# Gated attention output stored as two scaled fp16 halves and read back by transposing DMAs, with the transform matrices and the split of the output weights reordered

## The chip, the cores and the metric

The kernel runs on one core of a Trainium2 chip. A core has a matrix engine (TensorE, PE in the profile), three engines for elementwise work (VectorE or DVE, ScalarE or ACT, GpSimd or POOL), an engine that only issues transfers here (SyncE, SP) and sixteen DMA engines. Each engine works through its own queue of instructions in order; semaphores hold an instruction back until what it reads is there and what it overwrites is no longer needed. The metric is the device time of one execution in microseconds; lower is better.

## The reference

One block of a hybrid encoder: an RMS norm, one input projection of 1024 to 6144 columns, a Fourier branch, a dilated window attention branch, and one output projection with a residual. Sequence 2048, model width 1024, all fp32.

```python
hn = rms_norm(h, norm_w)
proj = hn @ w_in
u_f, g_f, q, k, v, g_a = jnp.split(proj, SPLIT_POINTS, axis=-1)
f = jnp.fft.fft2(u_f, axes=(1, 3), norm="ortho").real       # per group of 64 columns
f = jnp.einsum('bsgc,gcd->bsgd', f, w_fourier)
y_f = f * jax.nn.silu(g_f)                                  # 512 columns
...
o = jnp.sum(alpha[..., None] * jnp.stack(outs, axis=0), axis=0)   # three dilations, weighted
y_a = o * jax.nn.silu(g_a)                                  # 512 columns
h = h + jnp.concatenate([y_f, y_a], axis=-1) @ w_out
```

## The kernel before

All fp32 products are made of three products of a high and a low half: each operand is split into `hi` (rounded to a narrower type) and `lo` (the rest), and TensorE adds hi x hi, hi x lo and lo x hi. A split is one copy on ACT (hi) and one subtraction on DVE (lo).

The program has four stages. First come 192 items of the q, k, v projection (a row tile of 128 positions each, `inproj`), with the attention of earlier tiles laced in (lines 300 to 560). Then 48 items of the rest of the input projection (`chan`, `tok`): the Fourier gate, stored in DRAM as `SG`; the Fourier input `u`, from which `u_out` makes four folded arrays `F`; and the attention gate in 16 items q = 0 to 15 of 256 rows by 256 columns. Beside these items a generator (`og_all`) loads the three attention outputs of item q (`ot`) and weights and adds them into a tile `yo`. `ga_out` (L713) reads the gate from PSUM, computes silu (two ACT operations, one on DVE), multiplies `yo` by it, and puts q on a list; one item later `ya_st` (L720) stores `yo` in the DRAM array `YA`, 2048 x 512 fp32.

The third stage, from L1220 (`tail_`), is the Fourier transform over the sequence, as four transforms s = 0 to 3. `f_trans(s)` multiplies `F[s]` by a small block matrix in four blocks (PSUM tile `ptr`), and ACT (L776) and DVE (L777) split the result into `at`. `f_dft(s)` multiplies `at` by the transform matrix `dt` in four blocks `ct` of 128 channels (PSUM tile `pf`); s = 0 and 1 (256 columns a half, L807) and s = 2 and 3 (512 columns, L812). For even s, ACT copies the PSUM to `pe` (L816). For odd s, DVE forms the sum `t1` (L823) and the difference in `pe` (L824), and these multiply the gate `Y`, loaded from `SG`: the lower half (L826) on GpSimd, on DVE for s = 3, and the upper half (L827) on GpSimd. The matrix of transform s is loaded raw (`d_dma`, tile `dr`, two buffers) and split (`d_split`, ACT L759, DVE L760). `w_out` is loaded in sixteen pieces of 128 x 512 (`wor`, three buffers, L862), eight for each half of the output columns, and split by `wo_prep` (ACT L872, DVE L873). Both splits are generators, and `f_trans` and `f_dft` take steps from them (`fill`) at fixed places: this sets where the splits stand in the queues of ACT and DVE.

The fourth stage is the output projection, `o_mm(r)` for 16 row tiles r: 48 matmuls of 512 columns (L922) on the operand `mx`, whose columns 4 to 7 come from `YA` and 0 to 3 from `Y`. Before the matmuls of row r TensorE transposes row r+1 of `YA` (`ya`) in four pieces of 128 x 128 (L899, PSUM tile `pya`), and ACT (L900) and DVE (L901) split it into `mx`; L906 and L908 split the part of `Y`. Row 0 is prepared inside `f_dft(3)` (`o_in0`, `o_mix_a(0)`) and `o_mix_y(0)`. `o_in(r)` loads `ya` and the residual `xo` two rows ahead.

Instructions of one engine stand in the order in which the code calls them.

Of the kernel before, what the change touches and what calls it, by code (L numbers as in the profile page):

```python
# [92 lines left out]
class Kernel:  # L93
# [503 lines left out]
    def silu(self, out, ps, sb, e, z):  # L597
        V, A = self.nc.vector, self.nc.scalar
        A.activation(e, ps, AF.Tanh, scale=sb[:, 3:4])
        A.activation(z, ps, AF.Copy, scale=sb[:, 3:4])  # L600
        V.scalar_tensor_tensor(out, e, 1.0, z, op0=OP.add, op1=OP.mult)
# [86 lines left out]
    def og_all(self):  # L688
        V = self.nc.vector
        for q in range(2):  # L690
            self.og_load(q)
        yield
        for Q in range(8):
            if Q < 7:
                self.og_load(2 * Q + 2)
# [15 lines left out]

    def ga_out(self, u, q):
        ps = self.PS.pop((u, q))  # L713
        y = self.YO[q].rearrange("p r w -> p (r w)")
# [2 lines left out]
        self.nc.vector.tensor_tensor(y, y, e[:, 0], OP.mult)
# [27 lines left out]
    def d_dma(self, s):  # L745
        self.DR = [self.dp.tile([128, 2, 512], F32, name="dr", tag="dr", bufs=2) for _ in range(2)]
        for q in range(2):
            n = 512 if s > 1 else 256
# [40 lines left out]
    def f_dft(self, s, fill=iter(())):  # L789
# [6 lines left out]
        for ct in range(4):  # L796
# [29 lines left out]
            (V if s == 3 else G).tensor_tensor(lo, lo, t1, OP.mult)  # L826
# [37 lines left out]
    def wo_prep(self, nh, wo):  # L864
        nc = self.nc
        V, A = nc.vector, nc.scalar
        for k in range(KT):
# [4 lines left out]
            A.copy(wo[k][:, 0], raw)  # L872
            V.tensor_tensor(wo[k][:, 1], raw, wo[k][:, 0].bitcast(F32), OP.subtract)  # L873
# [17 lines left out]
    def o_mix_a(self, r):  # L891
# [5 lines left out]
        ps = (self.pso, self.psp)[r % 2].tile([128, 4, 128], F32, name="pya", tag="op"[r % 2])  # L897
        for k in range(4):
            nc.tensor.transpose(ps[:, k], ya[:, k * 128:k * 128 + 128], self.idf)  # L899
# [380 lines left out]
```

## Time and profile before

Three runs took 1420.67, 1421.93 and 1424.03 us; the median is 1421.93.

| | us |
|---|---|
| profiled execution | 1421.88 |
| its span | 1420.1 |
| attention and q, k, v projection (to about) | 908 |
| rest of the input projection, to | 1165.9 |
| Fourier transforms, to | 1231.2 |
| output projection, matmuls to | 1416.5 |
| TensorE busy | 1389.2 |
| DVE, ACT, GpSimd busy | 988.3, 739.9, 459.8 |

The profile names engines as above; PEld is TensorE's loading of weights. A row of the timeline gives the start in us, the time taken, the engine, the line, the operation, what it writes and reads, and how many instructions are merged; in brackets stands the idle time of the engine just ahead of it and what ended that. An engine's queue of transfers is marked with a q (SPq). A row of a group gives busy time and the mean of one in ns. The granted clock is the share of full speed that TensorE was given.

### The profile page before, as it was taken

How to read it: one execution, taken by the hardware profiler on the slowest of the kernel's cores; microseconds unless marked ns; L12 is line 12 of the kernel's file. 1: busy time of each engine (PE TensorE's matmuls, PEld its weight loads, DVE VectorE, ACT ScalarE, POOL GpSimd, SP SyncE). 2: the span in 40 equal slices, each digit the busy share in tenths (PEclk: the TensorE clock that was granted, in tenths of full speed). 3: DMA queues.
4: the chain of work that ended last, by engine and by line, in shares of the span. 5: the costliest groups of instructions: out<-in, count | busy, mean ns of one | idle time of the engine just before them, and what ended most of it. 6: DMA issues, size and time to landing. Idle time of an engine off the chain costs nothing.

```text
span 1420.1 us, 27783 instructions
## 1 busy us (share of the span) xinstructions
PE 1389.2 (98%) x9570; PEld 1027.6 (72%) x9570; DVE 988.3 (70%) x3143; ACT 739.9 (52%) x2079; POOL 459.8 (32%) x637
## 2 busy tenths in 40 slices
PE   5999999999999999999999999999999997999998
PEld 3666666667777777778888888754458687788887
DVE  7888888888878888888777777744488676511111
ACT  6867766676757666666666666554213134300110
POOL 0255544444444444444433333320010002211110
PEclk9999999999999999999999999999999999999999
DMA  6876867776776777686756565554434336333332
GB/s 223 203 135 129 151 122 143 126 139 131 142 134 129 149 122 147 121 151 121 151 104 134 97 128 102 131 125 117 144 120 138 107 97 253 104 111 111 112 119 74
DMA packets 407374, 188.14 MB, mean 132 GB/s; under 512 B 302720, under 2 KB 388928, under 8 KB 406720
## 3 DMA queue, kind: packets, MB, share of 16 engines
q1 hardware_dynamic: 378628, 173.36, 54.8%
q10 hardware_dynamic: 28604, 13.00, 3.9%
q8 instruction: 75, 1.23, 0.4%
q14 instruction: 67, 0.55, 0.1%
HBM read 72.37 MB, written 29.76 MB: 72 GB/s over the span
## 4 chain that ended last, share of the span: by engine, by line
PE 84%; DVE 5%; DMA 4%; issue 2%; POOL 2%; ACT 1%; SPq 1%; POOLq 0%; DVEq 0%; ACTq 0%
PE psq L312 45%; PE py L922 12%; PE psq L574 12%; PE psq L590 6%; PE pS L461 4%; PE po L527 2%; DMA wor<-in_w_out_dram 2%; PE po L528 1%; PE pS L449 1%; DVE xhl L223 1%; POOL ph L509 1%; PE pya L899 0%; DVE wo L873 0%; POOL hl L376 0%; PE ptr L774 0%
## 5 line engine op out<-in xcount | busy, mean ns | idle before, releaser
L312 PE MATMUL psq<-wh,xT 128*128 128x384 f16 x4608 | 787.0, 327 | 3.3 <-ACT wh L289 1.5
L312 PEld LDWEIGHTS <-xT 128*128 128x128 f16 x4608 | 540.2, 119 | 193.8 <-issue 4.6
L497 ACT ACTIVATE P<-pS,ob,kb 128x256 f32<-128x256 f32 (+1 forms) x384 | 199.7, 527 | 150.4 <-DVE ob L489 150.1
L509 POOL TENSOR_TENSOR ph<-P,ph 128x512 f16<-128x512 f32 x160 | 189.1, 1182 | 195.1 <-ACT ph L504 183.5
L922 PE MATMUL py<-wo,mx 128*128 128x512 f32 x768 | 181.3, 395 | 0.3 <-DVE mx L901 0.3
L365 POOL TENSOR_TENSOR qn<-qn,kb 128x128 f32<-128x128 f32 x192 | 84.7, 441 | 294.0 <-DVE qn L364 205.1
L574 PE MATMUL psq<-xT,wh 128*128 128x512 f16 x768 | 168.9, 379 | 0.0
L479 DVE CUSTOM_DVE_ANT_0 pS<-pS,bt 128x256 f32<-128x256 f32 (+1 forms) x384 | 147.8, 385 | 27.2 <-PE pS L449 18.9
L922 PEld LDWEIGHTS py<-wo,mx 128*128 128x128 f32 x768 | 143.2, 188 | 32.3 <-DVE mx L901 0.8
L376 POOL TENSOR_TENSOR hl<-qn,hl 128x256 f16<-128x256 f32 x192 | 134.1, 698 | 30.7 <-ACT hl L371 30.7
L574 PEld LDWEIGHTS <-wh 128*128 128x128 f16 x768 | 74.2, 98 | 86.9 <-issue 0.8
L925 DVE TENSOR_TENSOR xo<-xo,py 128x512 f32<-128x512 f32 x32 | 22.0, 688 | 139.1 <-PE py L922 139.1
L538 DVE TENSOR_REDUCE ob<-po 128x128 f32<-128x256 f32 (+1 forms) x160 | 75.2, 470 | 54.3 <-PE po L528 54.3
L504 ACT CAST ph<-P 128x512 f16<-128x512 f32 x160 | 99.1, 619 | 8.0 <-ACT P L497 1.3
L371 ACT CAST hl<-qn 128x256 f16<-128x256 f32 x192 | 77.1, 401 | 47.3 <-POOL qn L365 37.5
L332 DVE TENSOR_TENSOR vt<-psq,vt 128x128 f16<-128x128 f32 x192 | 55.0, 286 | 59.0 <-ACT vt L331 59.0
L331 ACT CAST vt<-psq 128x128 f16<-128x128 f32 x192 | 51.2, 266 | 83.0 <-PE po L528 83.0
L291 DVE SCALAR_TENSOR_TENSOR wh<-wr,nws,wh 128x384 f16<-128x384 f32 x128 | 88.0, 694 | 5.7 <-ACT wh L289 5.7
L900 ACT CAST mx<-pya 128x512 fp32r<-128x512 f32 x16 | 9.4, 587 | 148.2 <-issue 124.9
L590 PE MATMUL psq<-wh,xT 128*128 128x256 f16 x768 | 84.3, 273 | 0.0
L590 PEld LDWEIGHTS <-xT 128*128 128x128 f16 x768 | 75.1, 98 | 9.1
L323 ACT COPY raw<-psq 128x256 f32<-128x256 f32 x192 | 69.5, 362 | 21.8 <-PE psq L312 21.4
(158 smaller groups left out, 1777.9 us busy)
## 6 DMA issues: line engine op xcount, KB each, us to landing
wr<-in_w_in_dram SPq DMA_DIRECT2D x104, 192.0 KB, 2.9
ot<-O SPq DMA_DIRECT2D x16, 792.0 KB, 4.5
st<-st SPq DMA_DIRECT2D x96, 128.0 KB, 2.4
xs<-in_x_dram SPq DMA_DIRECT2D x16, 512.0 KB, 7.3
xo<-in_x_dram SPq DMA_DIRECT2D x16, 512.0 KB, 3.5
out_dram<-xo SPq DMA_DIRECT2D x15, 512.0 KB, 2.9
O<-ob ACTq DMA_DIRECT2D x108, 66.0 KB, 2.5
O<-ob ACTq DMA_DIRECT2D x32, 132.0 KB, 2.9
```

Source lines behind the costliest of these rows:

```text
L291: V.scalar_tensor_tensor(wh[:, 1, k - 1, :n], wr[k - 1], nws[:, k - 1:k], wh[:, 0, k - 1, :n], op0=OP.mult, op1=OP.subtract)
L312: nc.tensor.matmul(ps[:, :384], self.xtile(j, k, c, t), wh[:, l, k, :384], start=n == 0, stop=n == 23)
L365: G.tensor_tensor(qn[:, 2:4], qn[:, 2:4], self.kf[:, h0:h0 + 2], OP.mult)
L371: self.nc.scalar.copy(hl.rearrange("p a h l d -> p (a h) l d")[:, :, 0], qn)
L376: self.nc.gpsimd.tensor_tensor(hv[:, :, 1], qn, hv[:, :, 0], OP.subtract)
L479: V.tensor_tensor_reduce(out=sS[:, h, cs], in0=ps[:, h, cs], in1=bs, scale=1.0, scalar=-3.0e38, op0=OP.add, op1=OP.max, accum_out=mx[:, e, ...
L497: self.nc.scalar.activation(P[:, h, cs], sS[:, h, cs], AF.Exp, bias=ob[:, e, 130 + h:131 + h], scale=self.om[:, h0 + h:h0 + h + 1], accum_ ...
L504: self.nc.scalar.copy(ph[:, 0], P)
L509: self.nc.gpsimd.tensor_tensor(ph[:, 1], P, ph[:, 0], OP.subtract)
L574: nc.tensor.matmul(ps, wh[:, l, k, col * 128:col * 128 + 128], self.xT[:, j, k, ch * 512:ch * 512 + 512], start=n == 0, stop=n == 23)
L590: nc.tensor.matmul(ps[:, j * 256:j * 256 + 256], self.xT[:, i, k, r * 128:r * 128 + 128], wh[:, l, k, 128:384], start=n % 24 == 0, stop=n ...
L922: nc.tensor.matmul(ps[nh], m[:, j, k], wo[nh][k][:, l], start=(j, l, k) == (0, 0, 4), stop=(j, k) == (1, 3))
```

## The change

The gated attention output is no longer stored as fp32. `ya_scale` computes, once for each half of the columns, a power of two from the bound on the values (five DVE operations on 128 x 1) and its inverse; silu's factor is multiplied by the one, and rows 4 to 7 of the pieces of `w_out` by the other when they are split. One item after `ga_out`, `ya_split` makes two fp16 halves of `yo` (a copy on ACT, a subtraction on DVE); one item later `ya_st` stores both in `YA`, now 2 x 2048 x 512 fp16. The last two items are split after the loop, ahead of the transforms.

In the output projection two transposing DMAs for each row tile load the halves of `ya` with the columns on the partitions; ACT and DVE copy them into `mx`, and the transposes on TensorE go.

The third matrix (s = 2) gets its own raw buffers and its own split tile; it is loaded first in the tail, ahead of the first two pieces of `w_out` and of `Y`. The steps of the splits are dealt out anew: matrix 1 in `f_trans(0)`, matrix 2 and two pieces of `w_out` in `f_dft(0)`, none in `f_trans(2)` and `f_dft(1)`, one piece in `f_trans(3)`, the rest from `f_dft(2)` on. In `f_dft(3)` the lower product of the first two blocks goes to GpSimd. `yo` has 6 buffers for 8, `t1` 3 for 2.

```diff
-    def silu(self, out, ps, sb, e, z):
+    def silu(self, out, ps, sb, e, z, zs=None):
...
-        A.activation(z, ps, AF.Copy, scale=sb[:, 3:4])
+        A.activation(z, ps, AF.Copy, scale=sb[:, 3:4] if zs is None else zs)
...
-        self.silu(e[:, 0], ps, self.W[u][1], e[:, 0], e[:, 1])
+        if q % 8 == 0:
+            self.ya_scale(q // 8, self.W[u][1])
+        self.silu(e[:, 0], ps, self.W[u][1], e[:, 0], e[:, 1], self.YS[q // 8][:, 2:3])
         self.nc.vector.tensor_tensor(y, y, e[:, 0], OP.mult)
+        self.YL.append(q)
+
+    def ya_split(self, q):
+        y = self.YO.pop(q).rearrange("p r w -> p (r w)")
+        h = self.YH[q] = self.gp.tile([128, 2, 512], F16, name="yh", tag="yh", bufs=2)
+        self.nc.scalar.copy(h[:, 0], y)
+        self.nc.vector.tensor_tensor(h[:, 1], y, h[:, 0], OP.subtract)
         self.YD.append(q)
+
+    def ya_scale(self, hf, sb):
+        V = self.nc.vector
+        t = self.YS[hf] = self.sm.tile([128, 3], F32, name="ysc", bufs=2)
+        V.tensor_reduce(t[:, 1:2], self.IS[:, hf].rearrange("p c s h -> p (c s h)"), AX.X, OP.max)
+        V.scalar_tensor_tensor(t[:, 1:2], t[:, 1:2], 2.0 ** 16, sb[:, 1:2], op0=OP.mult, op1=OP.mult)
+        V.tensor_scalar(t[:, 0:1].bitcast(I32), t[:, 1:2].bitcast(I32), 0x7F800000, None, op0=OP.bitwise_xor)
+        V.tensor_scalar(t[:, 1:2], t[:, 1:2], 0.5, None, op0=OP.mult)
+        V.tensor_tensor(t[:, 2:3], t[:, 0:1], sb[:, 3:4], OP.mult)
 
     def ya_st(self, q):
         hf, g = divmod(q, 8)
-        dst = self.YA[g * 256:g * 256 + 256, hf * 256:hf * 256 + 256].rearrange("(r p) w -> p r w", p=128)
-        self.nc.sync.dma_start(dst, self.YO.pop(q))
+        h = self.YH.pop(q)
+        for l in range(2):
+            dst = self.YA[l, g * 256:g * 256 + 256, hf * 256:hf * 256 + 256].rearrange("(r p) w -> p r w", p=128)
+            self.nc.sync.dma_start(dst, h[:, l].rearrange("p (r w) -> p r w", r=2))
...
     def d_dma(self, s):
-        self.DR = [self.dp.tile([128, 2, 512], F32, name="dr", tag="dr", bufs=2) for _ in range(2)]
+        self.DR[s] = [(self.fp if s == 2 else self.dp).tile([128, 2, 512], F32, name="dr", tag="dr", bufs=2) for _ in range(2)]
...
-        d = (self.dp2 if s % 2 else self.dp).tile([128, 2, 4, 512], F32R, name="dt", tag="dt", bufs=1)
+        w = 512 if s else 256
+        d = (self.dp2 if s else self.dp).tile([128, 2, 4, w], F32R, name="dt", tag="dt2" if s == 2 else "dt", bufs=1)
...
-            (V if s == 3 else G).tensor_tensor(lo, lo, t1, OP.mult)
+            (V if s == 3 and ct > 1 else G).tensor_tensor(lo, lo, t1, OP.mult)
...
-            A.copy(wo[k][:, 0], raw)
-            V.tensor_tensor(wo[k][:, 1], raw, wo[k][:, 0].bitcast(F32), OP.subtract)
+            if k < 4:
+                A.copy(wo[k][:, 0], raw)
+                V.tensor_tensor(wo[k][:, 1], raw, wo[k][:, 0].bitcast(F32), OP.subtract)
+            else:
+                sc = self.YS[k // 2 - 2][:, 1:2]
+                A.activation(wo[k][:, 0], raw, AF.Copy, scale=sc)
+                V.scalar_tensor_tensor(wo[k][:, 1], raw, sc, wo[k][:, 0].bitcast(F32), op0=OP.mult, op1=OP.subtract)
...
-            self.OI[r] = ya = self.yp.tile([128, 512], F32, name="ya", tag="ya", bufs=3)
-            nc.sync.dma_start(ya, self.YA[r * 128:r * 128 + 128])
+            self.OI[r] = ya = self.yp.tile([128, 2, 4, 128], F16, name="ya", tag="ya", bufs=3)
+            for l in range(2):
+                nc.sync.dma_start(ya[:, l], self.YA[l, r * 128:r * 128 + 128], transpose=True)
...
-        for k in range(4):
-            nc.tensor.transpose(ps[:, k], ya[:, k * 128:k * 128 + 128], self.idf)
-        A.copy(m[:, 0, 4:8], ps)
-        V.tensor_tensor(m[:, 1, 4:8], ps, m[:, 0, 4:8].bitcast(F32), OP.subtract)
+        A.copy(m[:, 0, 4:8], ya[:, 0])
+        V.tensor_copy(m[:, 1, 4:8], ya[:, 1])
...
+                yl, self.YL = self.YL, []
                 if prev:
                     prev()
+                for q in yl:
+                    self.ya_split(q)
...
-        self.Y_dma()
+        self.d_dma(2)
         for k in range(2):
             self.wo_load(0, k)
+        self.Y_dma()
         flush = lambda g: [None for _ in g]
-        self.f_trans(0)
+        s1, s2, s3 = self.d_split(1, 3), self.d_split(2), self.d_split(3)
+        self.f_trans(0, s1)
         self.f_trans(1)
         ny = self.f_nyq()
-        s1, s2, s3 = self.d_split(1, 2), self.d_split(2, 3), self.d_split(3)
-        self.f_dft(0, chn(s1, w0))
-        self.f_trans(2, w0)
+        self.f_dft(0, chn(s2, cut(w0, 2)))
+        self.f_trans(2)
         self.f_nyq_mul(ny)
-        self.f_dft(1, chn(s2, w0))
+        self.f_dft(1)
...
-        self.f_trans(3, w0)
+        self.f_trans(3, cut(w0, 1))
...
-        self.f_dft(2, chn(s3, w0, w1))
+        self.f_dft(2, chn(cut(w0, 3), s3, w0, w1))
         self.f_dft(3, w1)
```

The changed lines' numbers move: L777 becomes L798, L760 L781, L824 L845, L826 L847, L873 L895 (L899 where it scales), L901 L927, L854 L875.

DVE's queue from the third `f_trans` through `f_dft(1)`, before (`at` are the splits of `f_trans(2)`, `wo` those of `w_out`, `dt` that of the third matrix, `t` and `pe` the results of the blocks of `f_dft(1)`):

```order
L777 TENSOR_TENSOR at<-ptr,at 128x512 x4
L873 TENSOR_TENSOR wo_17214<-wor,wo_17214 128x512 x3
L854 TENSOR_TENSOR Y<-Y,pm 128x4
L823 TENSOR_TENSOR t_17456<-pe,pf 128x512
L824 TENSOR_TENSOR pe<-pe,pf 128x512
L760 TENSOR_TENSOR dt<-dr,dt 128x1024 x2
L823 TENSOR_TENSOR t_17483<-pe,pf 128x512
L824 TENSOR_TENSOR pe<-pe,pf 128x512
L873 TENSOR_TENSOR wo_17214<-wor,wo_17214 128x512
L823 TENSOR_TENSOR t_17505<-pe,pf 128x512
L824 TENSOR_TENSOR pe<-pe,pf 128x512
```

The same place now:

```order
L781 TENSOR_TENSOR dt<-dr,dt 128x1024 x2
L895 TENSOR_TENSOR wo_17290<-wor,wo_17290 128x512 x2
L798 TENSOR_TENSOR at<-ptr,at 128x512 x4
L875 TENSOR_TENSOR Y<-Y,pm 128x4
L844 TENSOR_TENSOR t_17521<-pe,pf 128x512
L845 TENSOR_TENSOR pe<-pe,pf 128x512
L844 TENSOR_TENSOR t_17539<-pe,pf 128x512
L845 TENSOR_TENSOR pe<-pe,pf 128x512
L844 TENSOR_TENSOR t_17557<-pe,pf 128x512
L845 TENSOR_TENSOR pe<-pe,pf 128x512
```

The third matrix's split and every split of `w_out` are gone from between the blocks.

DVE's queue around `f_dft(3)`, before (all but the last piece of `w_out` are split ahead of the first block):

```order
L873 TENSOR_TENSOR wo_17560<-wor,wo_17560 128x512
L823 TENSOR_TENSOR t_17662<-pe,pf 128x512
L824 TENSOR_TENSOR pe<-pe,pf 128x512
L826 TENSOR_TENSOR Y<-Y,t_17662 128x512
L873 TENSOR_TENSOR wo_17560<-wor,wo_17560 128x512
L823 TENSOR_TENSOR t_17685<-pe,pf 128x512
L824 TENSOR_TENSOR pe<-pe,pf 128x512
L826 TENSOR_TENSOR Y<-Y,t_17685 128x512
L823 TENSOR_TENSOR t_17703<-pe,pf 128x512
L824 TENSOR_TENSOR pe<-pe,pf 128x512
L826 TENSOR_TENSOR Y<-Y,t_17703 128x512
L901 TENSOR_TENSOR mx_17669<-pya,mx_17669 128x512
```

The same place now (`wo_17580` to `wo_17616` are the second half of `w_out`, L927 the low half of row 0's operand):

```order
L895 TENSOR_TENSOR wo_17580<-wor,wo_17580 128x512 x2
L844 TENSOR_TENSOR t_17720<-pe,pf 128x512
L845 TENSOR_TENSOR pe<-pe,pf 128x512
L895 TENSOR_TENSOR wo_17581<-wor,wo_17581 128x512 x2
L844 TENSOR_TENSOR t_17750<-pe,pf 128x512
L845 TENSOR_TENSOR pe<-pe,pf 128x512
L899 SCALAR_TENSOR_TENSOR wo_17582<-wor,ysc,wo_17582 128x512 x2
L844 TENSOR_TENSOR t_17776<-pe,pf 128x512
L845 TENSOR_TENSOR pe<-pe,pf 128x512
L847 TENSOR_TENSOR Y<-Y,t_17776 128x512
L927 CAST mx_17728<-ya_17725 128x512
L899 SCALAR_TENSOR_TENSOR wo_17616<-wor,ysc,wo_17616 128x512 x2
```

Six pieces of `w_out` now stand between or behind the blocks, where there was one; two products went to GpSimd.

SP's queue from the load of the second matrix to the first load of `ya`, before:

```order
L750 DMA dr<-in_dft_dram 128x2x256 x2
L723 DMA YA<-yo 128x2x256 x3
L858 DMA Y<-SG 128x2048 x4
L862 DMA wor<-in_w_out_dram 128x512 x2
L750 DMA dr<-in_dft_dram 128x2x512 x2
L862 DMA wor<-in_w_out_dram 128x512 x7
L750 DMA dr<-in_dft_dram 128x2x512 x2
L862 DMA wor<-in_w_out_dram 128x512 x7
L878 DMA ya_17667<-YA 128x512
```

And now:

```order
L770 DMA dr<-in_dft_dram 128x2x256 x2
L743 DMA YA<-yh 128x2x256 x8
L770 DMA dr<-in_dft_dram 128x2x512 x2
L883 DMA wor<-in_w_out_dram 128x512 x2
L879 DMA Y<-SG 128x2048 x4
L770 DMA dr<-in_dft_dram 128x2x512 x2
L883 DMA wor<-in_w_out_dram 128x512 x10
L906 DMA_TRANSPOSE ya_17725<-YA 128x4x128 x2
L883 DMA wor<-in_w_out_dram 128x512 x4
```

The third matrix and two pieces of `w_out` moved ahead of `Y`; the transposing loads of row 0 stand ahead of the last four pieces.

More of the change, by code (lines that the diff above doesn't have):

```diff
@@ L702, in og_all @@
                 yield
-                y = self.gp.tile([128, 2, 256], F32, name="yo", tag="yo", bufs=8)
+                y = self.gp.tile([128, 2, 256], F32, name="yo", tag="yo", bufs=6)
                 yv = y.rearrange("p r (s w) -> p r s w", s=2)
@@ L821, in f_dft @@
             pe = self.PE_[:, ct]
-            t1 = self.fp.tile([128, 512], F32, name="t1", tag="t1", bufs=2)
+            t1 = self.fp.tile([128, 512], F32, name="t1", tag="t1", bufs=3)
             V.tensor_tensor(sh(t1), sh(pe), ps, OP.add)
@@ L877, in o_in0 @@
         ya = self.dp.tile([128, 2, 512], F32, name="ya0", tag="dr", bufs=2)[:, 0]
-        self.nc.sync.dma_start(ya, self.YA[0:128])
+        ya = ya.bitcast(F16).rearrange("p (l k n) -> p l k n", l=2, k=4)
+        for l in range(2):
+            self.nc.sync.dma_start(ya[:, l], self.YA[l, 0:128], transpose=True)
         m = self.ap.tile([128, 2, 4, 512], F32R, name="mx0", tag="at", bufs=2)
@@ L884, in o_in @@
         if r:
-            self.OI[r] = ya = self.yp.tile([128, 512], F32, name="ya", tag="ya", bufs=3)
-            nc.sync.dma_start(ya, self.YA[r * 128:r * 128 + 128])
+            self.OI[r] = ya = self.yp.tile([128, 2, 4, 128], F16, name="ya", tag="ya", bufs=3)
+            for l in range(2):
+                nc.sync.dma_start(ya[:, l], self.YA[l, r * 128:r * 128 + 128], transpose=True)
         xt = self.yp.tile([128, D], F32, name="xo", tag="xo", bufs=3)
@@ L949, in body @@
             self.SG = drm.tile([4, 128, S], F32, name="SG")
-            self.YA = drm.tile([S, 512], F32, name="YA")
+            self.YA = drm.tile([2, S, 512], F16, name="YA")
             self.KD = drm.tile([24, HD + 3], F32, name="KD")
-            for d in "W WL WS PS RAW QS QR HL TR ST QW VT BT SB PB PH OB OT DT AT OI MX OW XS XR XH XP YO WR XO".split():
+            for d in "DR YH YS W WL WS PS RAW QS QR HL TR ST QW VT BT SB PB PH OB OT DT AT OI MX OW XS XR XH XP YO WR XO".split():
                 setattr(self, d, {})
@@ L1043, in body @@
             ng = og = iter(())
-            self.YD = []
+            self.YD, self.YL = [], []
             for i in range(max(len(items) + 1, G + 32)):
@@ L1202, in body @@
             if tail:
-                for q in sorted(self.YO):
+                for q in self.YL:
+                    self.ya_split(q)
+                for q in sorted(self.YH):
                     self.ya_st(q)
@@ L1225, in tail_ @@
         w0 = self.wo_prep(0, wo[0])
-        chn = itertools.chain
-        self.Y_dma()
+        chn, cut = itertools.chain, itertools.islice
+        self.d_dma(2)
         for k in range(2):
             self.wo_load(0, k)
+        self.Y_dma()
         flush = lambda g: [None for _ in g]
-        self.f_trans(0)
+        s1, s2, s3 = self.d_split(1, 3), self.d_split(2), self.d_split(3)
+        self.f_trans(0, s1)
         self.f_trans(1)
         ny = self.f_nyq()
-        s1, s2, s3 = self.d_split(1, 2), self.d_split(2, 3), self.d_split(3)
-        self.f_dft(0, chn(s1, w0))
-        self.f_trans(2, w0)
+        self.f_dft(0, chn(s2, cut(w0, 2)))
+        self.f_trans(2)
         self.f_nyq_mul(ny)
-        self.f_dft(1, chn(s2, w0))
+        self.f_dft(1)
         w = [fpool.tile([128, 2, 2, 512], F32R, name=f"wo1{i}", tag=f"F{i}") for i in range(3)]
-        self.f_trans(3, w0)
+        self.f_trans(3, cut(w0, 1))
         w.append(fpool.tile([128, 2, 2, 512], F32R, name="wo13", tag="F3"))
```

5 lines of the change are left out of this document (2 added, 3 removed).

## The prediction

> **What bounds the kernel now.** I read the page's busy table first, then the chain that ended last in order of time, then TensorE's timeline around the places where that chain leaves TensorE.
>
> ```profile
> span 1420.1 us, 27783 instructions
> PE 1389.2 (98%) x9570; PEld 1027.6 (72%) x9570; DVE 988.3 (70%) x3143; ACT 739.9 (52%) x2079; POOL 459.8 (32%) x637
> ```
>
> TensorE (PE) is busy 98% of the span, so a gain must take work off TensorE or take away one of its few waits. The profiled execution took 1421.88 us: its span of 1420.1 plus 1.8 around it. The median of the three runs is 1421.93, so a difference in this execution can be read as a difference in the median.
>
> ```profile
> 1171.38 12.02 DMA wor<-in_w_out_dram
> 1184.79 4.46 DMA wor<-in_w_out_dram
> 1196.49 4.03 DVE dt L760 x2
> 1206.55 4.75 PE pf L812 x12
> 1244.65 11.07 PE py L922 x48
> 1394.30 22.16 PE py L922 x96
> ```
>
> The chain is TensorE nearly everywhere before 1171 us. Between 1171 and 1206, the stage of the Fourier transforms, it goes through loads of `w_out` and a split of the third matrix on DVE. From 1244 on it is the output projection.
>
> ```profile
> 1165.87 3.74 PE L774 MATMUL ptr<-BD,F 128*128 128x128 f32 x32
> 1194.54 2.84 PE L774 MATMUL ptr<-BD,F 128*128 128x128 f32 x24
> 1204.50 2.05 PE L774 MATMUL ptr<-BD,F 128*128 128x128 f32 x8 [7.12 <-DVE pe L824]
> 1206.20 21.88 PE L812 MATMUL pf<-dt,at 128*128 128x512 f32 x84
> 1231.16 0.63 PE L922 MATMUL py<-wo,mx 128*128 128x512 f32 x2
> 1238.00 0.66 PE L899 MATMUL pya<-idf,ya 128*128 128x128 f32 x4 [0.51 <-DMA ya<-YA]
> 1244.05 0.60 PE L899 MATMUL pya<-idf,ya 128*128 128x128 f32 x4
> 1255.56 0.60 PE L899 MATMUL pya<-idf,ya 128*128 128x128 f32 x4
> ```
>
> The one long wait is 7.12 us in `f_trans(3)`: its fourth block needs a PSUM tile that DVE still has to read (L824), and DVE stands in splits that wait for loads. It costs more than 7.12 us, as the windows of TensorE show (busy share, then granted clock, DMA share, GB/s):
>
> ```profile
> 1201.00:1202.00 1.00, 0.00 (x0) 0.50 0.22 80
> 1210.00:1211.00 1.00, 1.00 (x4) 0.65 0.00 0
> 1211.00:1212.00 1.00, 1.00 (x6) 1.00 0.00 0
> ```
>
> TensorE stops at 1197.4; about 3.3 us later the granted clock falls to a half, and it returns only near 1210.65, some 6.1 us after work resumed at 1204.50. So about 3.1 us of full-speed work are lost on top.
>
> **The change, part by part.**
>
> *Transposes removed from TensorE.* In the output projection a row tile takes 1255.56 - 1244.05 = 11.51 us. Without transposes it would be its 48 matmuls: 22.16 us for 96, or 11.08 for 48. Rows 1 to 15 save 15 x 0.43 = **6.5 us**, row 0's transposes in `f_dft(3)` 0.35. What replaces them: ACT copies fp16 halves from SBUF instead of PSUM (L926 for L900), DVE copies instead of subtracting; both had an 11 us row for about 1.3 us of such work, so this costs nothing in rows 2 to 15. Row 0 is another matter, below.
>
> *Loads by transposing DMAs.*
>
> ```profile
> st<-hl SPq DMA_TRANSPOSE x192, 2.8
> pt<-ph SPq DMA_TRANSPOSE x160, 3.7
> xT<-xhl SPq DMA_TRANSPOSE x12, 4.2
> ya<-YA SPq DMA_DIRECT2D x16, 256.0 KB, 3.3
> L514 SPq DMA_TRANSPOSE pt<-ph x160: 1231/1242/2427, 93.1 to 982.2; - x160
> ```
>
> No transposing load out of DRAM is in this trace, only out of SBUF. The same shape (`st<-hl`) lands in 2.8 us, a plain load of `YA` in 3.3, the largest transposing one in 4.2; an issue takes 1.24 us of SP. I take 3.5 us each; bounds 2.8 and 8.4 (the largest, twice, if the two halves run one after the other). Two per row are 2.5 us of SP's time in 11, and they go out two rows ahead, so they are hidden from row 2 on, even at 8.4.
>
> *The stall in `f_trans(3)`.* Between the two transforms DVE now has only the at-splits, the `Y` product and L844/L845 in its queue: the split of the third matrix goes into `f_dft(0)`, and of `w_out` only two pieces stand before `f_dft(1)`. What is late next is `Y`: L875 waits for all four 1 MB loads, which now go behind 1.0 MB of matrix and 0.5 MB of `w_out`.
>
> ```profile
> 1169.31 2.02 SPq L858 DMA_DIRECT2D Y<-SG  x4
> 1183.42 0.62 ACT L872 CAST wo<-wor 128x512 fp32r<-128x512 f32 x1 [2.69 <-DMA wor<-in_w_out_dram]
> ```
>
> Before, 4.2 MB of `Y` and 0.26 of `w_out` took from 1169.3 to 1183.4, say 12 us of moving and 2 of latency. Now 5.9 MB start about 1171.2 and land at about 1189, where TensorE brings L875's operand at about 1190. It fits, by one microsecond, and DVE then has 2 more before TensorE would notice. I take the whole stall as gone: **7.1 + 3.1 us**, and keep 0 to 3 us as the price of a late `Y`.
>
> *The split of y.* Sixteen times one ACT copy and one DVE subtract of 128x512. DVE's is 0.69 us by its neighbour L717, ACT's 0.62 by the same shape in L872.
>
> ```profile
> 1155.65 0.69 ACT L599 ACTIVATE ye<-psq,scb 128x512 f32<-128x512 f32 x1 [3.97 <-PE psq L590]
> 1167.41 0.69 DVE L601 SCALAR_TENSOR_TENSOR ye<-ye 128x512 f32<-128x512 f32 x1 [0.70 <-ACT ye L600]
> 1168.14 0.69 DVE L717 TENSOR_TENSOR yo<-yo,ye 128x512 f32<-128x512 f32 x1
> 1168.75 2.48 DVE L777 TENSOR_TENSOR at<-ptr,at 128x512 fp32r<-128x512 f32 x4
> ```
>
> In the gated-attention items ACT waits some 4 us of every 5.2 us item for TensorE, and ACT alone frees TensorE's PSUM there; so the splits cost nothing. ACT's copy now also waits for the store of two items earlier, which on SP can stand behind a load of `ot`; behind the copy on ACT are weight splits and the next gate, and 4 us are the cover. The last two splits have no such cover: both stand between L719 and the first at-split; the very last needs ACT's copy after L719 (0.6) and its own 0.69, and one earlier split fills the 0.70 idle. The second at-split ends near 1172.1 instead of 1170.0, and `f_trans(1)`, whose second block needs that PSUM at 1171.4, waits: **-1.0 us**. Its bounds are 0 and 2.1.
>
> *`w_out` moved later.* This is the new bill. Before, seven of the sixteen pieces were split ahead of `f_dft(1)`; now three ahead of `f_dft(2)`, and thirteen follow in 22 us through three load buffers, in DVE's queue ahead of L844 and of L927 that make row 0's operand. Each piece waits for the buffer of three pieces before.
>
> ```profile
> ACT wo L872 <- DMA wor<-in_w_out_dram: 11.6, 8, 2.7
> 1215.22 1.89 DVE L873 TENSOR_TENSOR wo<-wor,wo 128x512 fp32r<-128x512 f32 x3
> 1218.51 0.62 ACT L872 CAST wo<-wor 128x512 fp32r<-128x512 f32 x1 [2.61 <-DMA wor<-in_w_out_dram]
> 1225.35 1.74 POOL L827 TENSOR_TENSOR Y<-Y,pe 128x512 f32<-128x512 f32 x1 [16.16 <-DVE pe L824]
> 1225.78 1.85 DVE L873 TENSOR_TENSOR wo<-wor,wo 128x512 fp32r<-128x512 f32 x1
> ```
>
> From the split that frees a buffer (first of the three, done 1215.85) to the piece's arrival (1218.5) are 2.65 us; with ACT's 0.62 and DVE's 0.69 a buffer goes round in about 4.0 us. And a split that meets a GpSimd product takes 1.85 us instead of 0.69: it ends with GpSimd's. `f_dft(3)` now has six such GpSimd products, not four.
>
> ```profile
> 1204.14 1.29 POOL L826 TENSOR_TENSOR Y<-Y,t 128x512 f32<-128x512 f32 x1
> L823 DVE TENSOR_TENSOR t<-pe,pf 128x512 f32<-128x512 f32 x8 | 5.4, 678 | 0.0
> L759 ACT CAST dt<-dr 128x1024 fp32r<-128x1024 f32 x4 | 4.0, 1047 | 0.0
> ```
>
> The walk: without the stall `f_trans(3)` ends at 1199.4 (its start before, 1194.5, plus 3.8 for four blocks, plus 1.0), `f_dft(3)` begins at 1210.5 (48 matmuls, 11.08) and the projection at 1221.6. `f_dft(1)` gives GpSimd its first product at 1192.3; eight of 1.29 free the tile `pe` at 1202.7, and ACT, which waits for it, has the fourth piece near 1204, the sixth by 1206 and two matrix splits of 1.05 by 1208.2. DVE ends the matrix at 1209.9 (just in time for 1210.5) and the seventh piece at 1210.5. That frees the buffer of the tenth: arrival 1213.1, split 1214.4. L844 and L845 of the first block, 0.68 each, end at 1215.8. From there to L927 DVE has four splits, two more blocks of 1.4, a product and the copy, 6.5 us in all: 1222.3 at the earliest, some 4.3 us more if each of its SBUF operations first lets a GpSimd one finish (the 1.85 us row: 1.16 more for each of four splits, less what overlaps, and the copy). TensorE needs L927 at 1222.1, after two matmuls on the high half. So the wait is 0.2 to 4.5 us. I take 4.0, the contended end, since the one split in the trace that stood beside these products did collide. The last two pieces and `Y`'s part of row 0 then come in time, by 0.3 to 3 us: **-4.0**.
>
> *Row 0.* Before, 1231.16 to 1244.05 were 12.89 us for 11.08 of matmuls and 0.43 of transposes (counted); the rest, **1.4 us**, goes, as row 1's operand no longer stands in TensorE's queue. It lands near 1236, wanted at 1237.
>
> *At nothing:* `w_out`'s scale (same shape, one operand more), five 128x1 operations per half, buffer counts.
>
> **Sum:** 6.5 + 0.35 + 7.1 + 3.1 + 1.4 - 1.0 - 4.0 = 13.5 us less: 1421.9 - 13.5 = **1408.4 us**.
>
> [...]
>
> **The rivals.**
>
> *No new wait (0.20).* Loads land quicker or GpSimd and DVE miss each other; the wait is under 1.5 us. For it: DVE's own work would end at 1222.3, 0.2 us after it is wanted. Time 1404.4 to 1406.
>
> *The new wait halves the clock (0.17).* If TensorE idles over 3.3 us at the start of the projection as at 1197.4, 3.1 us are lost again: 1408.4 + 3.1 = 1411.5. The 4.0 us only slightly exceeds what the fall took, so it decides by where the idle time lies; the forecast assumes it doesn't.
>
> *The stall only moves (0.10).* `Y` lands 3 us late or more, GpSimd frees `pe` later, ACT splits the fourth matrix after 1210.5, and TensorE waits twice. The transposes' 6.9 us remain: 1413 to 1418.
>
> *Transposing loads from DRAM bind (0.07).* Against it: 2.8 to 4.2 us in the DMA table. Were a pair to occupy the DMA for P us, rows would take P instead of 11.08; from P = 11.08 + 13.5/15 = 12.0 us on it is slower than before. At P = 14 the time is 1408.4 + 15 x 2.9 = 1452.
>
> **How the numbers follow.** Forecast 0.46 (1406 to 1410), rivals 0.20, 0.17, 0.10, 0.07. The range 1403.5 to 1414 takes in the first three and the nearest part of the fourth. About 0.2% (2.8 us) is what a measurement of this kernel can tell from no change. Faster: all but the last and a corner of the fourth, 0.91; within 0.2%: 0.03; slower: 0.06.
>
> **What would show it.** Right: no row of `pya`; row tiles of 11.08 us; no idle before the fourth block of `f_trans(3)` and a granted clock of 1.00 through 1195 to 1220; under 2 us idle in `f_trans(1)`; TensorE at the projection near 1222, waiting there for DVE's L927. Wrong: a row tile above 11.1 us with a wait on `ya<-YA`; DVE idle before L875; TensorE waiting for `dt` at `f_dft(3)`; a new wait for ACT in the gated-attention items, where SP's stores stand behind loads of `ot`.

## The result: 10.7 us less, and the profile after

| | before | after |
|---|---|---|
| median, us | 1421.30 (4 runs, 1420.27 to 1424.03) | 1410.59 (4 runs, 1410.11 to 1411.41) |
| ratio after / before | | 0.9926, 95% interval 0.9913 to 0.9938 |
| profiled execution, us | 1421.88 | 1410.90 |

The time forecast was 1408.4 and the range 1403.5 to 1414. First the busy table of the changed kernel, then its TensorE timeline from the Fourier transforms to the projection (start, time taken, engine, line, operation; in brackets the idle time just ahead and what ended it).

```profile
span 1409.1 us, 27788 instructions
PE 1381.4 (98%) x9506; PEld 1020.7 (72%) x9506; DVE 992.7 (70%) x3167; ACT 748.7 (53%) x2095; POOL 459.7 (33%) x639
```

```profile
1166.72 3.74 PE L795 MATMUL ptr<-BD,F 128*128 128x128 f32 x32
...
1171.35 1.16 PE L795 MATMUL ptr<-BD,F 128*128 128x128 f32 x8
1172.71 2.94 PE L795 MATMUL ptr<-BD,F 128*128 128x128 f32 x24 [0.20 <-DVE at L798]
...
1195.62 3.73 PE L795 MATMUL ptr<-BD,F 128*128 128x128 f32 x32
1199.11 22.64 PE L833 MATMUL pf<-dt,at 128*128 128x512 f32 x96
1221.59 0.62 PE L948 MATMUL py<-wo,mx 128*128 128x512 f32 x2
1225.96 34.27 PE L948 MATMUL py<-wo,mx 128*128 128x512 f32 x136 [3.75 <-DVE mx L927]
```

The 64 transposes are gone (9506 matmuls for 9570), `f_trans(3)` runs its four blocks without a stop (1195.62), and the last two transforms follow without a break. The one new stop is at 1222.2, two matmuls into the projection, for 3.75 us. The windows of TensorE around it (stretch, its length in us, busy time with the matmuls begun, granted clock, DMA share, GB/s) show what it cost beyond itself:

```profile
1223.00:1224.00 1.00, 0.00 (x0) 1.00 0.00 0
1224.00:1225.00 1.00, 0.00 (x0) 0.89 0.00 0
1225.00:1226.00 1.00, 0.04 (x1) 0.50 0.00 0
...
1230.00:1231.00 1.00, 1.00 (x4) 0.50 0.61 111
1231.00:1232.00 1.00, 1.00 (x5) 0.69 0.96 387
1232.00:1233.00 1.00, 1.00 (x6) 1.00 1.21 230
```

The clock falls to a half at about 1224.8 (0.89 is 0.78 us at full speed and the rest at half) and is back at about 1231.6 (0.69 is 0.62 us at half speed and the rest at full). Work resumed at 1225.96, so 5.65 us ran at half speed: 2.8 us lost (the row's 136 matmuls took 34.27 us; at 11.08 for 48 they would take 31.4). The stop costs 3.75 + 2.8, about 6.6 us.

The span by stages, between the starts of the same rows in both profiles (the forecast from its own walk):

| stage | before | after | difference | forecast |
|---|---|---|---|---|
| up to `f_trans(0)` | 1165.87 | 1166.72 | +0.85 | 0 |
| `f_trans(0)` to `f_dft(2)` | 40.33 | 32.39 | -7.94 | -6.8 |
| `f_dft(2)` and `f_dft(3)` | 24.96 | 22.48 | -2.48 | -2.8 |
| projection, to the end | 188.94 | 187.51 | -1.43 | -3.9 |
| sum | 1420.10 | 1409.10 | -11.00 | -13.5 |

The first row lies within the scatter: the profiles of the twelve kernels below reach `f_trans(0)` between 1165.6 and 1167.7, the one without halves at 1166.19, and two with the halves at 1165.64 and 1165.79. The scatter arises ahead of what the change touches: the first matmul of the rest of the input projection starts at 908.2 before and 909.0 after, and from there to `f_trans(0)` both take 257.7 us. What was missed lies in the projection.

### The profile page after: what moved, and what is told of

Its sections match the earlier page's. It is cut to its first block, busy times and chain, and to the rows that moved or that the text cites. A ratio compares the mean times of both kernels' runs of the same rounds, so it can differ in the third digit from the quotient of the medians.

```text
span 1409.1 us, 27788 instructions
## 1 busy us (share of the span) xinstructions
PE 1381.4 (98%) x9506; PEld 1020.7 (72%) x9506; DVE 992.7 (70%) x3167; ACT 748.7 (53%) x2095; POOL 459.7 (33%) x639
## 4 chain that ended last, share of the span: by engine, by line
PE 82%; DVE 6%; issue 3%; DMA 3%; POOL 3%; ACT 2%; SPq 1%; POOLq 0%; DVEq 0%; ACTq 0%
PE psq L312 43%; PE py L948 13%; PE psq L574 12%; PE psq L590 5%; PE pS L461 3%; PE po L527 2%; PE po L528 1%; PE pS L449 1%; DVE xhl L223 1%; POOL ph L509 1%; DMA qw<-qw 1%; PE pf L828 1%; DMA wor<-in_w_out_dram 1%; POOL hl L376 1%; PE ptr L795 0%
## 5 line engine op out<-in xcount | busy, mean ns | idle before, releaser
L948 PEld LDWEIGHTS py<-wo,mx 128*128 128x128 f32 x768 | 146.1, 190 | 37.6 <-DVE mx L927 4.2
L951 DVE TENSOR_TENSOR xo<-xo,py 128x512 f32<-128x512 f32 x32 | 22.0, 686 | 144.1 <-PE py L948 144.1
L926 ACT CAST mx<-ya 128x512 fp32r<-128x512 f16 x16 | 9.9, 620 | 137.5 <-PE py L948 131.6
```

Of the source, the lines that this page charges most:

```text
L948: nc.tensor.matmul(ps[nh], m[:, j, k], wo[nh][k][:, l], start=(j, l, k) == (0, 0, 4), stop=(j, k) == (1, 3))
```

## Experiments

Theory after the result: the two halves of the change do what they should, and the loss at the projection comes from DVE's backlog in the last transform, where its operations on SBUF stand behind GpSimd's products. Rivals: the transposing loads cost something, the chain of `w_out` loads holds the operand back, the two products more on GpSimd do it, or the copy's place alone. The ratios are to the kernel before, timed beside each run with medians of 1421.3 to 1421.8 us.

### The change in its two halves

**halves_only:** fp16 halves and transposing loads, with `d_dma`, `d_split`, the fills, `t1` and the products as before the change.

```diff
-            (V if s == 3 and ct > 1 else G).tensor_tensor(lo, lo, t1, OP.mult)
+            (V if s == 3 else G).tensor_tensor(lo, lo, t1, OP.mult)
...
-        self.d_dma(2)
+        self.Y_dma()
         for k in range(2):
             self.wo_load(0, k)
-        self.Y_dma()
...
-        self.f_dft(0, chn(s2, cut(w0, 2)))
-        self.f_trans(2)
+        self.f_dft(0, chn(s1, w0))
+        self.f_trans(2, w0)
```

> Only the fp16 halves, the transposing loads and the scaled w_out; order, fills and buffers of the transforms as before. Theory (the two halves of the change add up): the transposes' 6.9 us and row 0's 1.4 us go, the stall of 7.1 us in f_trans(3) and the half clock after it stay, the last y-splits cost 0.4 us; about 1413.4 us (1412 to 1415), no wait of several us at the start of the projection. Rival (the transposing loads or the splits cost something that the new order hides): above 1416 us. Rival (the new order alone carries the gain): about 1421.

1418.09 us, ratio 0.9977 (0.9966 to 0.9987): 4.7 us above the forecast. The profile, an execution of 1416.82:

```profile
1207.08 2.05 PE L794 MATMUL ptr<-BD,F 128*128 128x128 f32 x8 [7.66 <-DVE pe L844]
...
1234.25 25.95 PE L947 MATMUL py<-wo,mx 128*128 128x512 f32 x111 [1.85 <-DVE mx L926]
...
1231.41 0.69 DVE L844 TENSOR_TENSOR pe<-pe,pf 128x512 f32<-128x512 f32 x1
...
1232.62 1.58 DVE L926 CAST mx<-ya 128x512 fp32r<-128x512 f16 x1
```

The old stall stays, as expected. But a wait for row 0's low half comes here too, without any new order: the copy takes 1.58 us. The execution profiled is the fastest of seven; the mean granted clock of the others was 0.995 or 0.996 where it was 0.997 here, so they ran longer at half speed than this profile shows.

**order_only:** the new order with `y` as fp32 and transposes on TensorE, that is, the change without `ya_split`, `ya_scale`, the scaled `w_out` and the transposing loads. Against the kernel before:

```diff
-            (V if s == 3 else G).tensor_tensor(lo, lo, t, OP.mult)
+            (V if s == 3 and ct > 1 else G).tensor_tensor(lo, lo, t, OP.mult)
...
-        self.f_dft(0, chn(s1, w0))
-        self.f_trans(2, w0)
+        self.f_dft(0, chn(s2, cut(w0, 2)))
+        self.f_trans(2)
```

> Only the new order: third matrix early, fills dealt anew, three t1 buffers, two products of the last transform on GpSimd; y stored as fp32, loaded plainly and transposed on TensorE as before. Theory: the stall in f_trans(3) and its half clock go (10.2 us), and the new wait at the start of the projection comes here as well, since it lies in DVE's queue ahead of row 0's low half: 2.5 to 3.2 us, with 0 to 2.7 us of half clock behind it; 1414 to 1417 us, and f_trans(1) loses nothing. Rival (the wait belongs to the transposing loads): no wait, 1411. Rival (the stall's end was worth less): above 1418.

1415.79 us, 0.9959 (0.9944 to 0.9973), within the theory's range; the wait of 2.20 us is below its 2.5 to 3.2. Its profile, DVE and GpSimd at row 0's low half, then TensorE:

```profile
1222.77 0.68 DVE L827 TENSOR_TENSOR Y<-Y,t 128x512 f32<-128x512 f32 x1
1223.37 0.68 DVE L902 TENSOR_TENSOR mx<-pya,mx 128x512 fp32r<-128x512 f32 x1
...
1222.93 1.74 POOL L828 TENSOR_TENSOR Y<-Y,pe 128x512 f32<-128x512 f32 x1 [1.94 <-DVE pe L825]
...
1224.11 6.94 PE L923 MATMUL py<-wo,mx 128*128 128x512 f32 x22 [2.20 <-DVE mx L902]
```

Here the low half is a subtraction from PSUM (`pya`) and takes 0.68 us while GpSimd's product runs. The copy from SBUF that replaces it took 1.58 beside such a product, and 0.43 where none ran. So the wait has two parts: the new order alone makes 2.2 us of it, and the halves make 1.55 more. Of these, 0.9 come from putting in place of an operation that did not collide one that does. The other 0.65 are there before the copy: with the halves DVE begins on the last transform's first block 7.8 us ahead of the projection, in order_only 8.4, where TensorE still does row 0's transposes (0.35 us) in between; the rest was not separated.

**halves_act:** halves_only, with row 0's low half copied by ACT:

```diff
-        V.tensor_copy(m[:, 1, 4:8], ya[:, 1])
+        if r == 0:
+            A.copy(m[:, 1, 4:8], ya[:, 1])
+        else:
+            V.tensor_copy(m[:, 1, 4:8], ya[:, 1])
```

> halves_only (order of the transforms as before, fp16 halves and transposing loads) with row 0's low half copied by ACT instead of DVE. Theory (halves_only came out 4.7 us above its forecast mostly because row 0's copy, now from SBUF to SBUF, collides with GpSimd and stands behind DVE's products, 1.85 us in its profile, and because the clock falls once more behind that wait in most of its runs): 1414.5 to 1416.3 us. Rival (the halves and their loads cost that much elsewhere): 1417.5 to 1418.5, no change.

1415.28 us, 0.9956 (0.9941 to 0.9971), in the theory's range. The copy explains 2.8 of the 4.7 us by which halves_only missed. Some 1.9 us remain. In this profile the part from 909.9, where the rest of the input projection begins (908.2 before), is 7.3 us shorter than before the change, for 7.9 forecast, and the stall of 7.64 us is 0.5 longer; what makes up the rest of the 1.9 was not separated.

### What makes the wait at the projection

**no_gpsimd:**

```diff
-            (V if s == 3 and ct > 1 else G).tensor_tensor(lo, lo, t1, OP.mult)
-            G.tensor_tensor(hi, hi, pe[:, 1 - par:], OP.mult)
+            if s < 3 or ct > 1:
+                (V if s == 3 else G).tensor_tensor(lo, lo, t1, OP.mult)
+            if s < 3:
+                G.tensor_tensor(hi, hi, pe[:, 1 - par:], OP.mult)
```

> The changed kernel without GpSimd's six products in the last transform (they are left out of the computation). Theory (collisions of DVE with GpSimd make most of the wait): the pairs of splits that took 3.0 us take 1.4, row 0's copy 0.43; the copy ends near 1222.5, the wait of 3.75 us falls under 1 us and the half clock behind it goes: 1404 to 1405.5 us. Rival (the loads of w_out through three buffers make it): the splits wait for their loads instead, the wait stays above 2.5 us, 1409 to 1410.5.

1404.20 us, 0.9878 (0.9863 to 0.9893). Groups of DVE's instructions between 1210 and 1226, of the changed kernel first, then of this one (count, busy time, mean of one in ns, idle before it):

```profile
L899 DVE SCALAR_TENSOR_TENSOR wo<-wor,ysc,wo 128x512 fp32r<-128x512 f32 x4 | 4.6, 1164 | 0.0
L895 DVE TENSOR_TENSOR wo<-wor,wo 128x512 fp32r<-128x512 f32 x4 | 4.4, 1114 | 2.0 <-ACT wo L894 2.0
...
L927 DVE CAST mx<-ya 128x512 fp32r<-128x512 f16 x1 | 1.6, 1580 | 0.0
```

```profile
L901 DVE SCALAR_TENSOR_TENSOR wo<-wor,ysc,wo 128x512 fp32r<-128x512 f32 x5 | 3.7, 747 | 1.0 <-ACT wo L900 1.0
...
L897 DVE TENSOR_TENSOR wo<-wor,wo 128x512 fp32r<-128x512 f32 x4 | 2.7, 685 | 2.0 <-ACT wo L896 2.0
...
L929 DVE CAST mx<-ya 128x512 fp32r<-128x512 f16 x1 | 0.4, 419 | 0.0
```

A split takes 0.69 to 0.75 us where 1.11 to 1.16 were the mean, the copy 0.42 instead of 1.58, and TensorE's wait is 0.29 us with the clock at 1.00 throughout. In the changed kernel a pair of splits and the copy end 0.3 to 0.6 us after the GpSimd product beside them:

```profile
1215.17 3.00 DVE L895 TENSOR_TENSOR wo<-wor,wo 128x512 fp32r<-128x512 f32 x2
1224.33 1.58 DVE L927 CAST mx<-ya 128x512 fp32r<-128x512 f16 x1
...
1215.81 1.81 POOL L848 TENSOR_TENSOR Y<-Y,pe 128x512 f32<-128x512 f32 x1
1223.88 1.74 POOL L848 TENSOR_TENSOR Y<-Y,pe 128x512 f32<-128x512 f32 x1 [1.95 <-DVE pe L845]
```

The 2.0 us in which DVE waits for loads are there in both and are not what TensorE waits for. Beside a GpSimd product the subtraction with one input in PSUM took 0.68 us (order_only) and the copy from SBUF 1.58; what makes the two differ was not shown by any run.

**four_buffers:** `wor` with four buffers, loads one piece further ahead; to make room, `ny` takes a buffer of `t1`.

```diff
-        ny = self.fp.tile([1, 512], F32, name="ny")
+        ny = self.fp.tile([128, 512], F32, name="ny", tag="t1", bufs=3)[0:1]
...
-        raw = self.WR[nh, k] = self.op.tile([128, 512], F32, name="wor", tag="wor", bufs=3)
+        raw = self.WR[nh, k] = self.op.tile([128, 512], F32, name="wor", tag="wor", bufs=4)
...
-            n = nh * KT + k + 2
+            n = nh * KT + k + 3
...
         self.Y_dma()
+        self.wo_load(0, 2)
```

> The changed kernel with four load buffers for w_out instead of three and the loads one piece further ahead; order of the splits as it is. Theory (collisions with GpSimd make the wait, the load chain only the 2.0 us in which DVE idles before 1213): DVE stays busy from 1213.4 on as before, row 0's copy comes 0.4 us sooner; 1409.5 to 1410.6 us. Rival (the chain of loads through three buffers makes the wait): the copy ends near 1222.5, 1404 to 1406 us.

1410.69 us, 0.9926 (0.9912 to 0.9941): no change. In its profile the wait is 3.42 us for 3.75. The load chain alone is not the cause.

**lo_on_dve:**

```diff
-            (V if s == 3 and ct > 1 else G).tensor_tensor(lo, lo, t1, OP.mult)
+            (V if s == 3 else G).tensor_tensor(lo, lo, t1, OP.mult)
```

> The changed kernel with all four low products of the last transform on DVE, as before the change (GpSimd has four products there instead of six). Theory (per block DVE pays GpSimd's remaining time either way: 3.0 us for two splits behind two products, or 0.6 for its own product and 2.5 for two splits behind one): no difference, 1409.8 to 1411.5 us. Rival (the two products more on GpSimd made the wait): 1407 to 1408.5. Rival (DVE's own work is the bound, each product on it costs 0.69): 1412 or more.

1409.54 us, 0.9917 (0.9903 to 0.9932), 0.3 us below the span that the theory gave and 1.05 below the changed kernel, with a wait of 3.77 us as before. The wait is not due to the two products more on GpSimd: the two splits behind two products take 3.0 us, DVE's own product and the two splits behind one take 0.6 + 2.45.

### Taking it away

**row0_early:**

```diff
-            if s == 3 and ct == 2:
+            if s == 3 and ct == 1:
                 self.o_mix_a(0)
```

> The changed kernel with row 0's two copies moved ahead of the w_out pieces of the second block of the last transform. Theory (DVE's whole backlog up to row 0's Y part is late, not the one copy): the wait at 1222 goes, but TensorE then waits in pieces for the last two w_out pieces (0.9 us) and for row 0's Y part (1.9 and 0.5 us), no idle stretch is long enough for the clock to fall; 3.3 us instead of 6.4: about 1407.5 us. Rival (the copy's place alone makes the wait): 1404 to 1405. Rival (the clock falls after these waits as well): about 1410.

1408.69 us, 0.9909 (0.9893 to 0.9926), 1.2 above the theory. TensorE waits in pieces, as the theory had it, but 0.38 and 1.87 us, and the clock does fall, at 1229.7 for 3.4 us:

```profile
1226.21 1.42 PE L948 MATMUL py<-wo,mx 128*128 128x512 f32 x5 [0.38 <-DVE wo L899]
1229.50 30.89 PE L948 MATMUL py<-wo,mx 128*128 128x512 f32 x125 [1.87 <-ACT mx L932]
```

**copy_on_act:** the changed kernel with the diff of halves_act.

> The changed kernel with row 0's low half copied by ACT instead of DVE, nothing else moved. Theory (DVE's queue ahead of the copy makes the first wait; behind it the backlog up to row 0's Y part is still late): no wait for the low half, the two last w_out pieces come in time, TensorE waits some 2 us for row 0's Y part near 1227, with up to 1.6 us of half clock behind it: 1406 to 1408.3 us. Rival (the copy alone is the cause): 1404 to 1405. Rival (something else holds the operand, the load of row 0 above all): 1409 or more.

1408.47 us, 0.9909 (0.9894 to 0.9923), 0.2 above the theory's range. TensorE in copy_on_act's profile:

```profile
1220.80 6.07 PE L951 MATMUL py<-wo,mx 128*128 128x512 f32 x24
1228.74 0.73 PE L951 MATMUL py<-wo,mx 128*128 128x512 f32 x2 [1.87 <-ACT mx L935]
1229.80 70.51 PE L951 MATMUL py<-wo,mx 128*128 128x512 f32 x298 [0.33 <-DVE mx L937]
```

With the first wait gone, TensorE does the 24 matmuls on row 0's part of `ya` and then waits for its part of `Y`, which stands at the end of the same backlog. Each of the two edits gains about 2 us of the 6.6; the rest only moves.

**pieces_early:** the diffs of four_buffers and of halves_act, and the splits of `w_out` dealt so that only four pieces, not six, stand in the last transform:

```diff
                     for _ in range(3 if s else 2):
                         next(fill, None)
+                elif s:
+                    next(fill, None)
                 continue
...
-            if ct < 3:
+            if ct < 2:
                 next(fill, None)
                 next(fill, None)
...
-        self.f_trans(3, cut(w0, 1))
+        self.f_trans(3, cut(w0, 2))
```

> The changed kernel with four load buffers, two w_out pieces more ahead of the last transform and none behind its third block, and row 0's low half copied by ACT. Theory (the whole loss is DVE's backlog in the last transform, where each of its SBUF operations first lets GpSimd's finish): TensorE has no wait over 0.5 us at the projection, the clock stays full, the same time as without GpSimd's products: 1404 to 1405.5 us. Rival (moving the splits forward only puts the wait before the last transform, at the fourth matrix): 1408 or more.

1404.63 us, 0.9885 (0.9870 to 0.9900): the best version, 6.0 us below the changed kernel and within 0.5 us of the one without GpSimd's products. TensorE, in its profile:

```profile
1220.66 6.25 PE L953 MATMUL py<-wo,mx 128*128 128x512 f32 x26
1227.23 73.16 PE L953 MATMUL py<-wo,mx 128*128 128x512 f32 x316 [0.32 <-DVE mx L939]
```

**early_dve_copy:** pieces_early without the diff of halves_act.

> pieces_early with row 0's low half copied by DVE again. Theory (the copy then stands behind the third block's product and a GpSimd product, however few w_out pieces are left): the copy ends near 1225, the wait of 3.4 to 3.8 us and the half clock are back, 1409.5 to 1411 us. Rival (taking the w_out pieces from in front of it was enough): 1404 to 1406.

1410.29 us, 0.9917 (0.9901 to 0.9934), within the theory's range, with a wait of 3.85 us: while the copy stands on DVE, fewer pieces in the last transform and a fourth buffer gain nothing. **early_three:** pieces_early without the diff of four_buffers.

> pieces_early with three load buffers, as in the changed kernel. Theory (the chain of loads through three buffers binds only ahead of 1213, where DVE idled 2.0 us): the splits ahead of the last transform end about 1 us later, row 0's Y part too; a wait of 0.3 to 1.5 us near 1227: 1404.6 to 1406.5 us. Rival (the fourth buffer doesn't matter): 1404.2 to 1404.8. Rival (it carries the gain): 1408 or more.

1407.38 us, 0.9901 (0.9886 to 0.9916): a miss by 0.9 us, in kind too. ACT in its profile, around the start of the projection:

```profile
1217.40 0.73 ACT L900 ACTIVATE wo<-wor,ysc 128x512 fp32r<-128x512 f32 x1 [1.93 <-DMA wor<-in_w_out_dram]
1220.98 1.34 ACT L900 ACTIVATE wo<-wor,ysc 128x512 fp32r<-128x512 f32 x2 [2.85 <-DMA wor<-in_w_out_dram]
1222.22 0.60 ACT L928 CAST mx<-ya 128x512 fp32r<-128x512 f16 x1
```

Row 0's copies stand behind the last two `w_out` pieces in ACT's queue, and these wait 2.85 us for loads; TensorE waits 2.20 us. So the load chain, which did not matter while DVE was late, binds once DVE is not: the fourth buffer is worth nothing by itself and 2.75 us in company. The ACT copy with the fourth buffer but without the pieces dealt anew was not run, so what the dealing adds is open.

### The transposing loads

**loads_twice:**

```diff
                 nc.sync.dma_start(ya[:, l], self.YA[l, r * 128:r * 128 + 128], transpose=True)
+            yb = self.yp.tile([128, 2, 4, 128], F16, name="yb", tag="yb", bufs=3)
+            for l in range(2):
+                nc.sync.dma_start(yb[:, l], self.YA[l, r * 128:r * 128 + 128], transpose=True)
```

> The changed kernel with a second pair of transposing loads per row, into a tile that nobody reads, issued behind the first pair (rows 1 to 15). Theory (the transposing loads are hidden: 2.5 us of SP's 11 per row, landed in 2.7 us): no change, 1410 to 1412 us, rows stay at 11.07 us. Rival (they bind, or they slow the other transfers): rows grow, a pair that costs 0.5 us more per row gives 7 us, 1417 or more.

1410.56 us, 0.9922 (0.9905 to 0.9938): hidden even when doubled. The DMA table has them at 2.7 us in the changed kernel, and at 3.0 and 2.7 here:

```profile
ya<-YA SPq DMA_TRANSPOSE x32, 2.7
```

```profile
ya<-YA SPq DMA_TRANSPOSE x32, 3.0
yb<-YA SPq DMA_TRANSPOSE x30, 2.7
```

## Why the prediction was right, and where it was off

- **Transposes, 6.5 + 0.35 us: right.** At the end of the changed kernel two row tiles run from one L951 to the fourth after it:

```profile
1383.36 0.69 DVE L951 TENSOR_TENSOR xo<-xo,py 128x512 f32<-128x512 f32 x1 [4.78 <-PE py L948]
...
1394.43 0.69 DVE L951 TENSOR_TENSOR xo<-xo,py 128x512 f32<-128x512 f32 x1 [4.78 <-PE py L948]
...
1405.49 0.69 DVE L951 TENSOR_TENSOR xo<-xo,py 128x512 f32<-128x512 f32 x1 [4.78 <-PE py L948]
```

  That is 11.07 us for a row, 11.08 forecast, 11.51 before.
- **Loads: right.** 2.7 us measured, 3.5 taken; doubled, they change nothing. Row 1's operand came at 1234, forecast near 1236, and TensorE did not wait for it.
- **Row 0, 1.4 us: right.** Without the 6.6 us of the stop the projection is 8.0 us shorter than before, for 6.45 + 1.4 forecast; in halves_act, which has no such stop, it is 8.0 us shorter too.
- **The stall, 7.1 + 3.1 us: right.** No idle time in `f_trans(3)`, clock 1.00 until the projection. `Y` was in time: L875 ran at 1190.34, with no wait for its loads. The third transform began at 1199.11 and the projection at 1221.59, against 1199.4 and 1221.6 forecast, though the first holds +0.85 of scatter.
- **The last two y-splits: half the size.** `f_trans(1)` takes 4.06 us (1171.35 to the next row at 1175.41) for 3.59 before, so 0.5 us, not 1.0.
- **The other y-splits and `ya_scale`, taken at nothing: right, though ACT does wait for them.** One sign of being wrong shows: ACT waits once for a store of `YA`, 1.9 us, and twice for `ya_scale`, 9.1 us in all. TensorE has no wait between 908 and 1165, so it costs nothing.
- **The wait for L927: right in place, cause and size.** 3.75 us, 4.0 forecast, with DVE's splits beside GpSimd paying (pairs of 3.00 and 3.08 us, 1.40 where no product ran). Of the two causes that the prediction set side by side, only the collisions were at work (no_gpsimd); the load chain was covered by them (four_buffers).
- **The clock: the step that failed.** The prediction took the half clock for a rival of 0.17, since 4.0 us "only slightly exceeds what the fall took", and "the forecast assumes it doesn't". It did fall, about 2.6 us after TensorE stopped, and 2.8 us were lost. The rival's time, 1411.5, is 0.6 from the execution profiled. By the prediction's own figures 4.0 us exceed the 3.3 that the fall took, and the sum left the loss out all the same. The error behind it was to read the 3.3 us from stop to fall in one trace (3.1 by finer windows: 1197.4 to 1200.46) as an idle time that must first be reached: where the fall came during the stop it came 2.4 us (four_buffers) to 3.7 us (halves_only) after TensorE stopped.
- **Row 0's copy "costs nothing in rows 2 to 15": right there; in row 0 its price was underrated.** Even without the new order it brought a wait of 1.85 us (halves_only). The prediction counted its collision only as the last part of the `w_out` pieces' backlog.
- **"The last two pieces and `Y`'s part of row 0 then come in time": true only because TensorE was late.** With the first wait removed, TensorE waits for them (row0_early, copy_on_act).

The forecast was 2.2 us below the median: +2.8 for the clock, -0.25 for the wait, -0.5 for the y-splits give +2.05. That the sum came so near is in part luck, as the smaller errors have the other sign.

## What to carry to other kernels

When a wait on a busy engine's queue is removed, look at everything that the queue must still deliver before the next stage, not at the instruction that is late first: here moving the copy alone gained a third, and the copy, the splits and a buffer together all of it. A subtraction from PSUM that becomes a copy within SBUF did not cost the same on VectorE while GpSimd was at work beside it (0.68 and 1.58 us here). Waits of 1.87 and 2.20 us on TensorE were each followed by 3.4 us at half the clock here (row0_early, order_only), and one of 1.85 us was not (halves_only): such a wait is to be priced with the clock that it may cost behind it.

## What the runs showed of the hardware

**The clock fell for shorter idle times than the stop of 7 us suggested.** In order_only TensorE idled 2.20 us, and lost clock after it had resumed:

```profile
1221.00:1222.00 1.00, 0.91 (x4) 1.00 0.73 234
...
1224.00:1225.00 1.00, 0.89 (x4) 1.00 0.00 0
1225.00:1226.00 1.00, 1.00 (x5) 0.65 0.06 16
1226.00:1227.00 1.00, 1.00 (x4) 0.50 0.00 0
...
1228.00:1229.00 1.00, 1.00 (x4) 0.65 0.18 41
1229.00:1230.00 1.00, 1.00 (x6) 1.00 0.90 274
```

It fell at about 1225.3 and rose at 1228.7, 3.4 us at half. The half-speed stretches lasted 3.4 us (order_only, copy_on_act, row0_early, lo_on_dve, early_three), 6.8 (the changed kernel, four_buffers, early_dve_copy, halves_only) or 10.2 (before, halves_act): one, two or three units of 3.41 us. In the profiles of the two kernels the last stretch at the full clock was a whole number of units too. In the changed kernel the clock fell once more at the end of the span, at 1409.10, 177.49 us after the rise at 1231.61, which is 52 units; before, it rose at 1210.70 and fell at 1418.90, 208.20 us later, which is 61.

So the length of a stop alone did not tell what it cost. In row0_early the stop of 1.87 us lies within the 3.41 us ahead of the fall (1226.27 to 1229.68), with TensorE at work in the other 1.5 us of them. The stop of 1.85 us in halves_only's profile, 1232.40 to 1234.25, cost no clock. By an estimate, units of 3.41 us counted on from the rise at 1209.90 in that profile, one ends at about 1233.8 and divides the stop, so that neither unit holds more than about 1.4 us of it; that this is why the clock stayed at full, no run shows. The same wait also cost one unit or two: lo_on_dve and the changed kernel both waited 3.8 us, and the one was at half speed for 3.4 us, the other for 6.8. The one was at work again 0.45 us before the fall, the other only 1.2 us after it.
